# Two passes instead of three in the output and down projection: the operand's high and low part side by side in one matmul of 512 columns

## The chip, the cores and the metric

The kernel runs on one core of a Trainium2 chip. The metric is the device time of one execution in microseconds (us). The engines are named as in the profile: PE (TensorE, the matmuls), PEld (its weight loads), DVE (VectorE), ACT (ScalarE), POOL (GpSimd) and SP (which issues the DMAs).

## What is computed

One layer of a decoder trunk, for 256 tokens of 2048 features, in float32:

```
h   = rms_norm(x) * gain + shift                 # gain, shift, g1, g2: c (1 x 2048) through w_ada
p   = h @ w_in                                   # 52 tiles of 128 columns
mix = [retention(p) | rwkv7(p) | moba(p)]        # 4 + 4 + 8 tiles of 128 features
x1  = x + g1 * (mix @ w_out)
h2  = rms_norm(x1) * gain + shift
u,v = conv3(h2 @ w_up)                           # 2 x 44 tiles of 128 columns
x2  = x1 + g2 * ((silu(u) * v) @ w_down)
out = rms_norm(x2)
```

## The kernel before

Features lie on the partitions and the 256 tokens along the free axis. All four products run tile by tile: a weight tile of 128 x 128 is the stationary operand, a feature tile of 128 x 256 (all tokens) the moving one, and the sum over feature tiles is kept in a PSUM bank. To keep float32 accuracy with the faster matmul type (float32r), weights and operands are both split into a high and a low part, and each weight tile takes three matmuls of 256 columns: high weight by high operand (line 1182), high weight by low operand (L1183), low weight by high operand (L1184). The product of both low parts is left out. A bank holds 512 float32 values on each partition; these products use its first half.

The weights come as a stream in the order of use, cut into chunks of 8 tiles (24 matmuls). For each chunk ACT writes the high part (`hi`, L454) and DVE the rest (`lo`, L455); `convert_until` does this two chunks ahead, into three buffers of each. There are 400 chunks: 104 for the input product, 32 for the output product (256 tiles), 176 for the up and 88 for the down product (704 tiles). Between the weights the stream also brings the 96 blocks of `w_ada`, which `ada_block` multiplies by the condition and sums on DVE (L408, 128 x 2048 elements each): the scales and shifts that the next norms need.

The operand of the output product comes from the three mixers. Retention and MoBA are done early; RWKV's steps alternate with chunks of the output product, and the hook at the 21st chunk waits until RWKV is finished. `split` writes the two parts of the result (`mxhi` with ACT, `mxlo` with DVE, L423 and L424). A column tile of the output product is summed in two parts, so there are 32 evacuations (`evac_out`, L1028, DVE: x = mm * g1 + x). The second of each is followed by the sum of squares for the next norm (`norm_acc`: ACT squares, POOL adds, and DVE does the last addition, L1042).

At the end of the output product the order is this. The first 64 tiles of the up product (8 chunks) work with x * gain before the norm is known (`xghi`, `xglo`, 258 columns). Meanwhile DVE finishes the sum of squares (`acc`), PE takes the mean (`nps`), DVE works out 1/sqrt in twelve small steps (`rsqrt`, L231 to L236), PE and ACT spread the result (`rs`), and DVE and ACT make the operand of the rest of the up product (`xn` and `hlo`, L434 and L436) and scale the early tiles (L1076). Then come the up product's other chunks with `hhi` and `hlo`.

The operand of the down product is `ghi` and `glo`, its 16 column tiles are summed over 44 feature tiles each without a break, and `evac_down` (L1123) ends each one.

The program is written as one loop over the chunks (L1156 on). A scheduler then puts each engine's instructions in a fixed order, by its own estimate of when each could run; each engine executes its own list in that order. So the order of `lo`, `ada` blocks, evacuations and norm steps on DVE is not written by hand, and it changes when the program changes.

Of the kernel before, what the change touches and what calls it, by code (L numbers as in the profile page):

```python
# [8 lines left out]
F32 = mybir.dt.float32  # L9
# [14 lines left out]
# input projection tiles, 128 columns each: 0-15 RWKV (r, k, v, [wd, wa, wg, wg]),  # L24
# 16-27 retention (q, k, v, g), 28-51 MoBA (q, k, v of a head side by side)
# [33 lines left out]
    # input projection: S tiles stay open over all k, a k tile at a time; others are visited for some k tiles  # L59
# [29 lines left out]
    # output projection: retention and half of MoBA, then the other half of MoBA, and RWKV  # L89
# [68 lines left out]
# parts of w_ada, blocks of 128 channels  # L158
ADA = {"mix_shift": 0, "mix_gain": 16, "g1": 32, "ffn_shift": 48, "ffn_gain": 64, "g2": 80}
RAWB, EXTRA, CONVB, AHEAD = 3, 2, 3, 2  # L160
# blocks of the modulation in the last part of the input projection, four of the output and three of the up projection
LATE_ADA = (18, 3, 3, 2, 0, 7, 7, 8)
# column pairs of the up projection that begin with x * gain, before the norm of x is known
EARLY = 8
# chunks of the output projection that wait for MoBA, for RWKV, and that begin the FFN; steps of the mixers per chunk
WAITS = (7, 20, 28)
TASKS = 5
# blocks of weights that may wait in the arena, up to a chunk
# [3 lines left out]
def trunk(tc, A):  # L172
# [12 lines left out]
    # one piece of memory in turn for more blocks of weights, the mixers, and the up projection  # L185
# [16 lines left out]
    def s4(name, dt=F32):  # L202
        return arena.tile([128, 4, T], dt, tag="s4", name=nm(name))

# [21 lines left out]
    def rsqrt(x, w):  # L226
        """x ** -0.5 on [128, w], three Newton steps from an integer estimate."""
# [11 lines left out]
    # ---- constants and vectors  # L239
# [16 lines left out]
    # ---- x, its mean square, and x / rms  # L256
# [4 lines left out]
    # ---- the stream of weights  # L261
# [17 lines left out]
    def begun(m, f):  # L279
        """blocks of a product before the first tile of k tile f or later"""  # L280
# [29 lines left out]
    def lead():  # L310
        """blocks of weights that may wait in the arena"""
# [3 lines left out]
    def place(it):  # L315
        """memory for the next block, in one piece or two; None while it is all in use"""
# [29 lines left out]
    # silu(c) along the free axis of all partitions  # L346
# [24 lines left out]
    def norm_bcast(ms, name):  # L371
        """rms of the tokens (mean squares in ms[:, 0:2]) -> 1/rms on all partitions, [128, 256] in PSUM"""
# [26 lines left out]
    # ---- modulation: w_ada has its output channels on the partitions  # L399
# [870 lines left out]
```

## Time and profile before

| | |
|---|---|
| runs (device time of one execution) | 1331.02, 1331.79, 1333.01 us; median 1331.79 |
| the profiled execution, first to last instruction (span) | 1329.3 us |
| PE busy | 1290.8 us, 97% |
| DVE busy | 1034.6 us, 78% |
| ACT busy | 648.6 us, 49% |
| output product, first to last matmul | 397.9 to 552.4 us |
| early tiles of the up product (258 columns), up to | 577.8 us |
| other tiles of the up product, up to | 1061 us |
| down product, up to | 1314 us |
| last norm and store | 1314 to 1329.3 us |

The profile gives the profiled execution's span alone. The median of the timed runs is 2.5 us above it, so a change of the span by d puts the median at about 1331.8 + d. Times within the span are us from its first instruction. A matmul's recorded duration (0.28 us) is longer than the distance to the next one, since consecutive matmuls overlap; the distance between two starts is what a matmul costs in a row of them.

### The profile page before, as it was taken

To read this page: it belongs to the slowest core of one execution; us is meant where nothing else is said; L and a number is where in the kernel's file an instruction comes from. 1 tells how busy PE (TensorE), PEld (TensorE's weight loads), DVE (VectorE), ACT (ScalarE), POOL (GpSimd) and SP (SyncE) were. 2 spreads that over 40 slices of the span, in tenths; PEclk is the share of its full clock that TensorE was granted. 3 is DMA by queue.
4 is the path that set the end of the run, shared out by engine and by line. 5 is a ranking of instruction groups with operands and counts; after the bars stand their busy time and mean duration, and the time that the engine had idled before them with its cause. 6 is when DMAs were issued, how large, how long until landed. Compare 5 with 4: busy or idle time off the path is not lost.

```text
span 1329.3 us, 25320 instructions
## 1 busy us (share of the span) xinstructions
PE 1290.8 (97%) x10524; PEld 1272.4 (96%) x10524; DVE 1034.6 (78%) x1606; ACT 648.6 (49%) x1043; POOL 40.2 (3%) x41
## 2 busy tenths in 40 slices
PE   5899999999999999999999999999999999999996
PEld 5899999999999999999999999999999999999995
DVE  7888989999897579999777898888866666566444
ACT  3454435566346324565445655656554544434341
POOL 0000000000000001400000000000000000000000
PEclk8999999999999899999999999999999999999998
DMA  9998887775537279677775565565655577767551
GB/s 386 365 349 317 314 316 286 285 271 194 217 128 253 96 251 402 210 281 297 270 285 188 173 210 191 190 210 175 219 190 183 206 247 270 267 241 271 187 191 64
DMA packets 49939, 320.56 MB, mean 241 GB/s; under 512 B 5536, under 2 KB 6048, under 8 KB 15776
## 3 DMA queue, kind: packets, MB, share of 16 engines
q1 hardware_dynamic: 48528, 315.10, 66.2%
q0 software_dynamic: 1008, 3.67, 0.7%
q8 instruction: 82, 1.34, 0.4%
q14 instruction: 33, 0.27, 0.1%
q10 hardware_dynamic: 288, 0.17, 0.0%
HBM read 316.83 MB, written 2.10 MB: 240 GB/s over the span
## 4 chain that ended last, share of the span: by engine, by line
PE 90%; DVE 7%; issue 2%; ACT 1%; DMA 0%; POOL 0%; DVEq 0%; ACTq 0%; POOLq 0%
PE mm L1182 26%; PE mm L1184 26%; PE mm L1183 26%; DVE raw L408 2%; DVE lo L455 1%; PE pair L1182 1%; PE pair L1184 1%; PE pair L1183 1%; PE xx L774 1%; PE sp L919 1%; PE sp L933 1%; PE u L911 1%; PE akv L784 0%; PE yps L913 0%; PE xx L775 0%
## 5 line engine op out<-in xcount | busy, mean ns | idle before, releaser
L455 DVE TENSOR_TENSOR lo<-raw,hi 128x1024 fp32r<-128x1024 f32 x400 | 488.7, 1224 | 201.9 <-ACT hi L454 200.8
L454 ACT CAST hi<-raw 128x1024 fp32r<-128x1024 f32 x400 | 418.3, 1047 | 449.5 <-PE mm L1183 373.3
L1182 PE MATMUL mm<-hhi,hi 128*128 128x256 f32 x2016 | 571.7, 284 | 0.0
L1184 PE MATMUL mm<-hhi,lo 128*128 128x256 f32 x2016 | 571.1, 283 | 0.5 <-DVE lo L455 0.5
L1183 PE MATMUL mm<-hlo,hi 128*128 128x256 f32 x2016 | 571.3, 283 | 0.0
L1184 PEld LDWEIGHTS mm<-hhi,lo 128*128 128x128 f32 x2016 | 386.6, 192 | 1.3 <-DVE lo L455 0.9
L1182 PEld LDWEIGHTS mm<-hhi,hi 128*128 128x128 f32 x2016 | 386.8, 192 | 0.6 <-issue 0.3
L1183 PEld LDWEIGHTS mm<-hlo,hi 128*128 128x128 f32 x2016 | 386.8, 192 | 0.3
L408 DVE SCALAR_TENSOR_TENSOR raw<-raw,cb 128x2048 f32<-128x2048 f32 x96 | 221.7, 2310 | 5.2 <-DMA raw<-w_ada 5.2
L1184 PE MATMUL mm<-ghi,lo 128*128 128x256 f32 x704 | 199.1, 283 | 0.0
L1182 PE MATMUL mm<-ghi,hi 128*128 128x256 f32 x704 | 198.8, 282 | 0.0
L1183 PE MATMUL mm<-glo,hi 128*128 128x256 f32 x704 | 198.5, 282 | 0.0
L1183 PEld LDWEIGHTS mm<-glo,hi 128*128 128x128 f32 x704 | 134.6, 191 | 0.0
L1182 PEld LDWEIGHTS mm<-ghi,hi 128*128 128x128 f32 x704 | 134.5, 191 | 0.0
L1184 PEld LDWEIGHTS mm<-ghi,lo 128*128 128x128 f32 x704 | 134.4, 191 | 0.0
L1182 PE MATMUL mm<-mxhi,hi 128*128 128x256 f32 x256 | 75.1, 293 | 1.0 <-DVE x L1028 0.9
L1184 PE MATMUL mm<-mxhi,lo 128*128 128x256 f32 x256 | 73.2, 286 | 0.4 <-DVE lo L455 0.4
L1183 PE MATMUL mm<-mxlo,hi 128*128 128x256 f32 x256 | 73.5, 287 | 0.0
L1042 POOL TENSOR_TENSOR acc<-acc,nsq 128x256 f32<-128x256 f32 x28 | 34.2, 1221 | 848.8 <-ACT nsq L1041 848.6
L1182 PE MATMUL pair<-hhi,hi 128*128 128x256 f32 x160 | 45.7, 298 | 7.1 <-ACT hi L454 5.2
L1182 PEld LDWEIGHTS mm<-mxhi,hi 128*128 128x128 f32 x256 | 49.7, 194 | 2.8 <-DVE x L1028 1.1
L1184 PEld LDWEIGHTS mm<-mxhi,lo 128*128 128x128 f32 x256 | 49.7, 194 | 0.5 <-DVE lo L455 0.5
(292 smaller groups left out, 1304.8 us busy)
## 6 DMA issues: line engine op xcount, KB each, us to landing
raw<-w_ada SPq DMA_DIRECT2D x96, 1024.0 KB, 5.1
raw<-w_up SPq DMA_DIRECT2D x67, 1024.0 KB, 4.9
raw<-w_in SPq DMA_DIRECT2D x52, 1024.0 KB, 5.8
raw<-w_down SPq DMA_DIRECT2D x44, 1024.0 KB, 5.0
raw<-w_up SPq DMA_DIRECT2D x42, 512.0 KB, 8.3
raw<-w_out SPq DMA_DIRECT2D x18, 512.0 KB, 8.8
raw<-w_out SPq DMA_DIRECT2D x7, 1024.0 KB, 4.9
x<-xT SPq DMA_DIRECT2D x4, 512.0 KB, 5.5
```

The costliest lines, as they stand in the source:

```text
L408: V.scalar_tensor_tensor(raw, raw, 1.0, cb, op0=OP.mult, op1=OP.mult, accum_out=m)
L454: S.copy(flat(hi), src)
L455: V.tensor_tensor(flat(lo), src, flat(hi).bitcast(F32), op=OP.subtract)
L774: PE.matmul(ps[:, T * i:T * i + 128], L[pb, f, sl], At[pb, f, sl], start=True, stop=True)
L911: PE.matmul(ups[pb, 128 * f:128 * f + 128], M1[:, f, ts], sb[:, f], start=True, stop=True)
L919: PE.matmul(sp[:, fs], kT[pb, h, fs], vT[pb, h, fs], start=(f == 0), stop=False, skip_group_check=True)
L933: PE.matmul(sp[:, fs], bT[pb, h, fs], U[pb, h, fs], start=False, stop=True, skip_group_check=True)
L1042: (V if t == NF - 1 else G).tensor_tensor(norm["acc"], norm["acc"], sq, op=OP.add)
L1182: PE.matmul(ps, whi[:, j], hi, start=first and not (two and t % 2), stop=False, skip_group_check=two)
L1183: PE.matmul(ps, whi[:, j], lo, start=False, stop=False, skip_group_check=two)
L1184: PE.matmul(ps, wlo[:, j], hi, start=False, stop=last, skip_group_check=two)
```

## The change

`pairs` lays the high and the low part of a feature tile next to each other, so that both are one run of 512 columns. In the output and down products (`WIDE`) the high weight tile is then loaded once and multiplied by all 512 columns, into a whole bank; the low weight tile still takes the 256 columns of the high part, into the bank's first half. Two matmuls and two weight loads stand where three and three stood, with as many columns in all. The evacuation adds the two halves of the bank to x one after the other, so it takes two DVE instructions instead of one. `split` writes RWKV's share in two pieces instead of one, since a pair of feature tiles is now one buffer. Input and up product only address their operand differently.

```diff
+WIDE = ("out", "down")
...
+    def pairs(name, tile_of=None):
+
+        shape = lambda x: x.rearrange("p (f h) t -> p f h t", h=2)
+        return [shape((tile_of or s4)(name, F32R)) for _ in range(2)]
...
     def split(g, sl, src):
...
         if g not in MX:
-            MX[g] = s4("mxhi", F32R), s4("mxlo", F32R)
-        hi, lo = (flat(x)[:, sl] if isinstance(sl, slice) else x[:, :, sl[0]] for x in MX[g])
-        S.copy(hi, src)
-        V.tensor_tensor(lo, src, hi.bitcast(F32), op=OP.subtract)
+            MX[g] = pairs("mx")
+        f, n, ts = sl
+        while n:
+            w = min(n, 2 - f % 2)
+            x = MX[g][f // 2][:, f % 2:f % 2 + w]
+            hi, lo = x[:, :, 0, ts], x[:, :, 1, ts]
+            S.copy(hi, src[:, 0:w])
+            V.tensor_tensor(lo, src[:, 0:w], hi.bitcast(F32), op=OP.subtract)
+            src = src[:, w:]
+            f, n = f + w, n - w
...
     def evac_out(t, part, ps):
         dst = x1[t // 4][:, t % 4]
-        V.scalar_tensor_tensor(dst, ps, mod["g1"][:, t:t + 1], dst, op0=OP.mult, op1=OP.add)
+        for h in range(2):
+            V.scalar_tensor_tensor(dst, ps[:, T * h:T * h + T], mod["g1"][:, t:t + 1], dst, op0=OP.mult, op1=OP.add)
...
     def evac_down(t, part, ps):
         dst = x1[t // 4][:, t % 4]
-        V.scalar_tensor_tensor(dst, ps, mod["g2"][:, t:t + 1], dst, op0=OP.mult, op1=OP.add)
+        for h in range(2):
+            V.scalar_tensor_tensor(dst, ps[:, T * h:T * h + T], mod["g2"][:, t:t + 1], dst, op0=OP.mult, op1=OP.add)
...
-            PE.matmul(ps, whi[:, j], hi, start=first and not (two and t % 2), stop=False, skip_group_check=two)
-            PE.matmul(ps, whi[:, j], lo, start=False, stop=False, skip_group_check=two)
-            PE.matmul(ps, wlo[:, j], hi, start=False, stop=last, skip_group_check=two)
+            if m in WIDE:
+
+                x = operands(m, k)
+                PE.matmul(ps.rearrange("p (h t) -> p h t", h=2), whi[:, j], x, start=first, stop=False,
+                          skip_group_check=True)
+                PE.matmul(ps[:, 0:T], wlo[:, j], x[:, 0], start=False, stop=last, skip_group_check=True)
+            else:
...
```

The scheduler's order changes with it, at three places. In the rows below `mm` is a bank of a product, `mx`, `xg` and `h` its operands (of the output product, of the up product's first and of its other tiles), `hi` and `lo` the weights, `raw` a block as loaded, and numbers tell buffers apart.

PE, at the end of the output product, where the up product's first tiles follow; before:

```order
L1182 MATMUL mm_6203<-mxhi_5208,hi_6110 128x256
L1183 MATMUL mm_6203<-mxlo_5209,hi_6110 128x256
L1184 MATMUL mm_6203<-mxhi_5208,lo_6111 128x256
L1182 MATMUL mm_6251<-xghi,hi_6148 128x258
L1183 MATMUL mm_6251<-xglo,hi_6148 128x258
```

and now:

```order
L1199 MATMUL mm_5985<-mx_5153,hi_5908 128x512
L1201 MATMUL mm_5985<-mx_5153,lo_5909 128x256
L1204 MATMUL mm_6031<-xghi,hi_5940 128x258
L1205 MATMUL mm_6031<-xglo,hi_5940 128x258
L1206 MATMUL mm_6031<-xghi,lo_5941 128x258
```

A tile of the output product has two matmuls instead of three; the up product keeps three. Over the program PE has 960 matmuls and as many weight loads fewer, one for each of the 256 + 704 tiles. Also, 141 of the 256 tiles stood ahead of RWKV's last transposes (`yt`) on PE before, and 170 do now.

DVE, at the last evacuations of the output product; before:

```order
L1028 SCALAR_TENSOR_TENSOR x_4723<-mm_6165,mod_g_160,x_4723 128x256
L455 TENSOR_TENSOR lo_6187<-raw_5641,hi_6186 128x1024
L1028 SCALAR_TENSOR_TENSOR x_4723<-mm_6190,mod_g_160,x_4723 128x256
L1028 SCALAR_TENSOR_TENSOR x_4723<-mm_6203,mod_g_160,x_4723 128x256
L416 TENSOR_TENSOR mod_ffn_shift<-mod_ffn_shift,vec 128x1
L455 TENSOR_TENSOR lo_6225<-raw_5677,hi_6224 128x1024
L1042 TENSOR_TENSOR acc_5803<-acc_5803,nsq_6221 128x256
```

and now:

```order
L468 TENSOR_TENSOR lo_5973<-raw_5530,hi_5972 128x1024
L1042 SCALAR_TENSOR_TENSOR x_4723<-mm_5976,mod_g_160,x_4723 128x256
L1042 SCALAR_TENSOR_TENSOR x_4723<-mm_5985,mod_g_160,x_4723 128x256
L1042 SCALAR_TENSOR_TENSOR x_4723<-mm_5976,mod_g_160,x_4723 128x256
L1042 SCALAR_TENSOR_TENSOR x_4723<-mm_5985,mod_g_160,x_4723 128x256
L468 TENSOR_TENSOR lo_6005<-raw_5559,hi_6004 128x1024
L1056 TENSOR_TENSOR acc_5656<-acc_5656,nsq_6001 128x256
```

Each tile is evacuated twice. From RWKV's last split up to the last evacuation DVE's list had 18 evacuations, 5 `ada` blocks, 13 `lo` of weights, 5 `xglo` and 4 small instructions; it now has 32, 1, 11, 5 and none.

DVE, within the norm's twelve small steps, which follow; before:

```order
L235 TENSOR_TENSOR rsa_6234<-rsa_6234,m_6231 128x2
L408 SCALAR_TENSOR_TENSOR raw_6318,mod_ffn_gain<-raw_6318,cb 128x2048
L236 SCALAR_TENSOR_TENSOR rsy_6233<-rsa_6234,rsy_6233 128x2
L455 TENSOR_TENSOR lo_6283<-raw_5678,hi_6282 128x1024
L234 SCALAR_TENSOR_TENSOR rsa_6234<-rsy_6233 128x2
L455 TENSOR_TENSOR lo_6325<-raw_5744,hi_6324 128x1024
L235 TENSOR_TENSOR rsa_6234<-rsa_6234,m_6231 128x2
L410 SCALAR_TENSOR_TENSOR mod_ffn_gain<-mod_ffn_gain,bias_164,vec 128x1
L236 SCALAR_TENSOR_TENSOR rsy_6233<-rsa_6234,rsy_6233 128x2
```

and now:

```order
L415 SCALAR_TENSOR_TENSOR raw_6098,mod_ffn_gain<-raw_6098,cb 128x2048
L241 SCALAR_TENSOR_TENSOR rsa_6014<-rsy_6013 128x2
L468 TENSOR_TENSOR lo_6206<-raw_5740,hi_6205 128x1024
L242 TENSOR_TENSOR rsa_6014<-rsa_6014,m_6011 128x2
L468 TENSOR_TENSOR lo_6245<-raw_5741,hi_6244 128x1024
L243 SCALAR_TENSOR_TENSOR rsy_6013<-rsa_6014,rsy_6013 128x2
L417 SCALAR_TENSOR_TENSOR mod_ffn_gain<-mod_ffn_gain,bias_164,vec 128x1
L241 SCALAR_TENSOR_TENSOR rsa_6014<-rsy_6013 128x2
L415 SCALAR_TENSOR_TENSOR raw_6199,mod_ffn_shift<-raw_6199,cb 128x2048
L242 TENSOR_TENSOR rsa_6014<-rsa_6014,m_6011 128x2
L415 SCALAR_TENSOR_TENSOR raw_6280,mod_ffn_gain<-raw_6280,cb 128x2048
L243 SCALAR_TENSOR_TENSOR rsy_6013<-rsa_6014,rsy_6013 128x2
```

`ada` blocks have moved from ahead of the last evacuation to behind it. From the last evacuation up to the `lo` of the third chunk that needs `hhi`, DVE's list had 2 `ada` blocks, 9 `lo`, 13 `xn` and `hlo`, 4 scalings of early tiles, `acc` and 14 small instructions; it now has 7, 9, 14, 4, one and 19. The step `rs` on PE, which waits for the last of the twelve, has moved: 75 of the 258-column matmuls stood between the last matmul of the output product and it, now 129 do.

## Rows read from the trace of the kernel before

**Rows 1.** The page, busy time of the engines, share of the span, instructions.

```profile
PE 1290.8 (97%) x10524; PEld 1272.4 (96%) x10524; DVE 1034.6 (78%) x1606; ACT 648.6 (49%) x1043; POOL 40.2 (3%) x41
```

**Rows 2.** The page, shares of the chain that ended last, by engine.

```profile
PE 90%; DVE 7%; issue 2%; ACT 1%; DMA 0%; POOL 0%; DVEq 0%; ACTq 0%; POOLq 0%
```

**Rows 3.** Stretches: length, busy us of PE, PEld, DVE, ACT, POOL; clock, DMA share.

```profile
513.60:553.30 39.70, 38.75 (x321) 38.36 (x320) 39.01 (x52) 21.10 (x32) 16.75 (x13) 1.00 0.87 331
600.00:700.00 100.00, 100.00 (x836) 100.00 (x835) 79.41 (x93) 50.89 (x80) 0.00 (x0) 1.00 0.77 279
1200.00:1300.00 100.00, 100.00 (x838) 100.00 (x837) 50.97 (x48) 40.88 (x48) 6.42 (x6) 1.00 0.59 200
```

**Rows 4.** The chain by line, window 531 to 553 us.

```profile
by line: DVE lo L455 34.6%; issue 24.4%; DVE x L1028 19.7%; DVE raw L408 16.5%; ACT hi L454 4.8%; DVE mod_ffn_gain L410 1.4%; DVE mod_ffn_shift L416 1.0%
```

**Rows 5.** The chain by line, window 1061 to 1314 us (down projection).

```profile
by line: PE mm L1184 33.5%; PE mm L1182 33.3%; PE mm L1183 33.3%
```

**Rows 6.** Timeline, down projection, PE and PEld: start, us, what.

```profile
1150.02 0.28 PE L1183 MATMUL mm<-glo,hi 128*128 128x256 f32 x1
1150.02 0.19 PEld L1184 LDWEIGHTS mm<-ghi,lo 128*128 128x128 f32 x1
1150.14 0.28 PE L1184 MATMUL mm<-ghi,lo 128*128 128x256 f32 x1
1150.14 0.19 PEld L1182 LDWEIGHTS mm<-ghi,hi 128*128 128x128 f32 x1
```

**Rows 7.** Timeline, PE, plain float32 matmuls.

```profile
415.21 1.06 PE L858 MATMUL y<-R,bd 128*128 128x128 f32 x8
416.10 0.60 PE L603 MATMUL mo_o<-mo_ptb,mo_vs 128*128 128x256 f32 x2
```

**Rows 8.** DVE groups by form, window 513.6 to 553.3 us: busy, mean ns.

```profile
L455 DVE TENSOR_TENSOR lo<-raw,hi 128x1024 fp32r<-128x1024 f32 x13 | 16.3, 1255 | 0.3 <-ACT hi L454 0.3
L408 DVE SCALAR_TENSOR_TENSOR raw<-raw,cb 128x2048 f32<-128x2048 f32 x5 | 12.8, 2570 | 0.0
L1028 DVE SCALAR_TENSOR_TENSOR x<-mm,mod_g,x 128x256 f32<-128x256 f32 x18 | 8.3, 472 | 0.4 <-PE mm L1184 0.4
```

**Rows 9.** Timeline, PE, end of the output and start of the up projection.

```profile
552.39 0.28 PE L1184 MATMUL mm<-mxhi,lo 128*128 128x256 f32 x1
...
577.78 0.28 PE L1182 MATMUL mm<-hhi,hi 128*128 128x256 f32 x1
...
583.54 0.28 PE L1182 MATMUL mm<-hhi,hi 128*128 128x256 f32 x1
```

**Rows 10.** Timeline, DVE, from the last evacuation of the output projection on.

```profile
552.76 0.47 DVE L1028 SCALAR_TENSOR_TENSOR x<-mm,mod_g,x 128x256 f32<-128x256 f32 x1
...
555.64 0.43 DVE L1042 TENSOR_TENSOR acc<-acc,nsq 128x256 f32<-128x256 f32 x1 [0.62 <-POOL acc L1042]
556.82 0.16 DVE L374 TENSOR_SCALAR m<-nps 128x2 f32<-128x2 f32 x1 [0.76 <-PE nps L1046]
557.02 0.17 DVE L231 TENSOR_SCALAR rsy<-m 128x2 int32<-128x2 int32 x1
557.22 0.17 DVE L232 TENSOR_SCALAR rsy<-rsy 128x2 int32<-128x2 int32 x1
...
557.70 2.28 DVE L408 SCALAR_TENSOR_TENSOR raw<-raw,cb 128x2048 f32<-128x2048 f32 x1
...
564.80 0.88 DVE L434 SCALAR_TENSOR_TENSOR xn<-x,mod_ffn_gain,rs_ffn 128x256 f32<-128x256 f32 x2
565.59 1.22 DVE L1076 TENSOR_TENSOR up<-up,rs_ffn 128x1024 f32<-128x1024 f32 x1
...
573.20 1.22 DVE L455 TENSOR_TENSOR lo<-raw,hi 128x1024 fp32r<-128x1024 f32 x1 [0.17 <-ACT hi L454]
...
581.50 2.35 DVE L455 TENSOR_TENSOR lo<-raw,hi 128x1024 fp32r<-128x1024 f32 x2
```

**Rows 11.** Timeline, DVE, the last evacuation of the down projection.

```profile
1314.51 0.48 DVE L1123 SCALAR_TENSOR_TENSOR x<-mm,mod_g,x 128x256 f32<-128x256 f32 x1 [6.45 <-PE mm L1184]
```

More of the change, by code (lines that the diff above doesn't have):

```diff
@@ L429, in h_tile @@
         if g not in H:
-            H[g] = s4("hhi", F32R), s4("hlo", F32R)
-        hi, lo = H[g]
+            H[g] = pairs("h")
+        hi, lo = (H[g][j // 2][:, j % 2, i] for i in range(2))
         gain, shift = (mod[kind + n][:, f:f + 1] for n in ("_gain", "_shift"))
@@ L434, in h_tile @@
         V.scalar_tensor_tensor(xn, XN[kind][g][:, j], gain, RS[kind], op0=OP.mult, op1=OP.mult)
-        S.activation(hi[:, j], xn, AF.Identity, bias=shift)
-        V.scalar_tensor_tensor(lo[:, j], xn, shift, hi[:, j].bitcast(F32), op0=OP.add, op1=OP.subtract)
+        S.activation(hi, xn, AF.Identity, bias=shift)
+        V.scalar_tensor_tensor(lo, xn, shift, hi.bitcast(F32), op0=OP.add, op1=OP.subtract)
     hooks = {}
@@ L556, in retention @@
             done()
-            split(0, slice(512 * hh, 512 * hh + 512), flat(mixed[:, 2 * hh:2 * hh + 2]))
+            split(0, (2 * hh, 2, slice(0, T)), mixed[:, 2 * hh:2 * hh + 2])
             yield 1 - hh
@@ L605, in moba @@
         yield
-        split(g, slice(T * (h % 4), T * (h % 4) + T), o[:, 0:256])
+        split(g, (h % 4, 1, slice(0, T)), o[:, None, 0:256])
         done()
@@ L976, in rwkv @@
             done()
-            split(1, (sl,), mixed[:, :, sl])
+            split(1, (0, 4, sl), mixed[:, :, sl])
             yield
@@ L1114, in evac_up @@
         if g not in GT:
-            first = lambda n: tail[0].tile([128, 4, T], F32R, tag="gt", name=nm(n))
-            GT[g] = (first("ghi"), first("glo")) if g < 2 else (s4("ghi", F32R), s4("glo", F32R))
-        hi, lo = GT[g]
-        S.copy(hi[:, j], v)
-        V.tensor_tensor(lo[:, j], v, hi[:, j].bitcast(F32), op=OP.subtract)
+            first = lambda n, dt: tail[0].tile([128, 4, T], dt, tag="gt", name=nm(n))
+            GT[g] = pairs("g", first if g < 2 else s4)
+        hi, lo = (GT[g][j // 2][:, j % 2, i] for i in range(2))
+        S.copy(hi, v)
+        V.tensor_tensor(lo, v, hi.bitcast(F32), op=OP.subtract)
     def evac_down(t, part, ps):
         dst = x1[t // 4][:, t % 4]
-        V.scalar_tensor_tensor(dst, ps, mod["g2"][:, t:t + 1], dst, op0=OP.mult, op1=OP.add)
+        for h in range(2):
+            V.scalar_tensor_tensor(dst, ps[:, T * h:T * h + T], mod["g2"][:, t:t + 1], dst, op0=OP.mult, op1=OP.add)
         norm_acc(t, dst)
@@ L1138, in operands @@
             k = RANK[k]
-        hi, lo = src[k // 4]
-        return hi[:, k % 4], lo[:, k % 4]
+        return src[k // 4][k % 4 // 2][:, k % 2]
     evac = {"in": evac_in, "out": evac_out, "up": evac_up, "down": evac_down}
@@ L1178, in trunk @@
             early = m == "up" and t % NP < EARLY and k < 4
-            ps = opened[t][:, 0:T + 2] if early else opened[t][:, 0:T]
-            hi, lo = (x[:, k] for x in XG) if early else operands(m, k)
+            ps = opened[t] if m in WIDE else opened[t][:, 0:T + 2] if early else opened[t][:, 0:T]
             two = t in both
-            PE.matmul(ps, whi[:, j], hi, start=first and not (two and t % 2), stop=False, skip_group_check=two)
-            PE.matmul(ps, whi[:, j], lo, start=False, stop=False, skip_group_check=two)
-            PE.matmul(ps, wlo[:, j], hi, start=False, stop=last, skip_group_check=two)
+            opens = first and not (two and t % 2)
+            if m in WIDE:
[4 more added lines that the diff above has]
+            else:
+                hi, lo = (x[:, k] for x in XG) if early else (operands(m, k)[:, i] for i in range(2))
+                PE.matmul(ps, whi[:, j], hi, start=opens, stop=False, skip_group_check=two)
+                PE.matmul(ps, whi[:, j], lo, start=False, stop=False, skip_group_check=two)
+                PE.matmul(ps, wlo[:, j], hi, start=False, stop=last, skip_group_check=two)
             if last:
```

## The prediction, made before the changed kernel ran

> **What bounds the kernel now.** First the page: PE is busy 97% of the span [rows 1] and holds 90% of the chain that ended last, DVE 7% [rows 2]. An average hides the stages, so next the stretches: from 600 us on PE is busy 100% and DVE has slack, while between RWKV's last split (513.6) and the last evacuation of the output product (553.3) DVE is busy 39.0 of 39.7 us [rows 3]. There the chain's largest shares are DVE's: the weights' `lo`, the evacuations, the `ada` blocks [rows 4]. In the down product the chain is PE's three matmul lines, a third each, and nothing else [rows 5]. So two stages are to be judged: down, where a nanosecond per tile on PE is a nanosecond of the end, times 704; and the passage from output to up product, where DVE's list decides. In these stretches the granted clock is 1.00 [rows 3], the 2.4 GHz level, at which 256 columns at one per cycle would take 106.7 ns.
>
> **The down product.** Matmuls start 0.12 us apart, and the next weights' load starts together with each matmul [rows 6]; the stretch of 100 us with 838 recorded matmuls [rows 3] gives 119.3 ns, a few missing records aside, so I use 120. A tile is 3 x 120 = 360 ns now. Afterwards it is one pass of 512 columns plus one of 256, the latter 120 as now. No float32r pass of 512 columns stands in the trace, so I bound it. Above: twice a pass, 240, if the 13.3 ns over 106.7 go with the columns. Below: the nearest row with as many cycles is plain float32 with 256 columns, which streams at half the rate: two of them last 0.60 us, one record of such is 0.38, so 0.22 lies between them, while eight with 128 columns last 1.06 us, (1.06 - 0.28) / 7 = 0.11 apiece [rows 7]. From 0.11 to 0.22 the stream doubles, and what lies over 106.7 and 213.3 is 3 to 7 ns in both: there the excess belongs to the instruction, not to the columns. So I take a fixed excess: 213.3 + 13.3 = 227 ns, a tile of 347, 13.3 ns saved, 704 x 13.3 = **-9.4 us**. The ends are a tile of 216 + 120 = 336 (24 ns, -16.9 us), with the float32 row's excess alone, and 360 (0).
>
> The Trainium skill ("TensorE: Matmul & The Clock Gate", section "Back-to-back issue gap") gives N/2.4 + 2.5 ns for the gap at full clock, 216 ns for 512 columns. It also gives 109 for 256, where the rows above show 120, so applied to both passes it would leave only 2.5 ns per tile, 1.8 us in the stage, to be saved.
>
> Evacuations in down go from 16 to 32. DVE is half idle there [rows 3], so all but the last are hidden; the cover would be gone only if DVE filled. The last tile's second instruction lies on the path to the final norm: one costs 0.47 to 0.48 us [rows 10, 11], **+0.4** for a second behind it.
>
> **The output product and its passage to the up product.** PE alone would save 256 x 13.3 = 3.4 us here. But the end of this stage is set by DVE, whose list is the same set of work in another order. I go through it in two pieces.
>
> *RWKV's split to the last evacuation.* On PE 170 tiles instead of 141 now stand ahead of RWKV's last transposes. The extra 29 cost 29 x 0.347 = 10.1 us, the other 141 save 141 x 0.0133 = 1.9, so RWKV's split comes 8.2 later, near 521.8. After it, DVE's list loses 4 `ada` blocks of 2.57 us, 2 `lo` of 1.26 and four small instructions, and gains 14 evacuations of 0.47 [rows 8]: 39.0 - 10.3 - 2.5 - 0.8 + 6.6 = 32.0. The last evacuation ends near 521.8 + 32.0 = 553.8 instead of 553.2 [rows 10]: **+0.6**. PE's own work would let it end 3.4 earlier, which bounds this term below; the pieces of RWKV's split and waits put its upper end at about +3.
>
> *The last evacuation to the third chunk that needs the normed operand.* Before, DVE ended the last evacuation at 553.2 and the third chunk's `lo` (the first of the pair that starts at 581.50) at 582.7, 29.5 us later [rows 10]. PE came to that chunk at 583.54 and to its third matmul, the first that reads `lo`, 0.24 later [rows 9]: a reserve of 1.1 us, no more. The list now holds 5 more `ada` blocks in this piece. One takes 2.2 us of the queue (2.28 recorded, less its overlap with the next) [rows 10]. With one more `xn` (0.88 for two, so 0.4) and five small steps (0.2 between starts) [rows 10] that is 11.0 + 0.4 + 1.0 = 12.4 us, while what PE does meanwhile is the same 190 early matmuls and two chunks. Each `ada` block stands between dependent steps of 1/sqrt, so it delays `rs`, then the operand, then the `lo` behind them; the waits for POOL and PE of 0.62 and 0.76 us [rows 10] come ahead of most of them and hide one block at best in part. What is late next is PE: it should stand first at `rs`, then at the first chunks of `hhi`. Shift: 12.4 - 1.1 = **+11.3**. After that the up product is PE alone at 100% [rows 3] with its three passes unchanged, and never gets this back. The blocks that were taken forward are missing later, where DVE had slack: nothing gained. The extra 32 evacuations and the two pieces of the split are counted in the lists above; DMAs are the same in number.
>
> **Sum.** -9.4 + 0.4 + 0.6 + 11.3 = +2.9 us on the profiled execution's span of 1329.3, 1332.2. The runs' median, 1331.8, lies 2.5 above the span; with the same difference **1334.7 us**. A measurement of this kernel can tell about 0.2%, 2.7 us, from no change: 1329.1 to 1334.5 counts as the same, so this sits on the edge of it.
>
> **Rivals.**
> 1. *The excess goes with the columns* (0 to 4 ns saved per tile). For it: 256-column passes show 13 ns over the stream where float32 shows 3 to 7, and what differs is the rate at which the operand is read. Against: the float32 rows' fixed excess. Then down gives 0 to -2.8, RWKV's split comes about 10 later, the last evacuation +2, and the passage still +11.3: 1331.8 - 1.4 + 0.4 + 2 + 11.3 = 1344.
> 2. *The excess is that of the load beside the stream and vanishes behind a long pass* (336 ns a tile): the kernel is faster. The place is down: 704 x 24 = -16.9. The split comes 29 x 0.336 - 141 x 0.024 = 6.4 later, the last evacuation at 552.0, -1.2; passage +11.3, tail +0.4: 1331.8 - 6.4 = 1325.4. It decides from 17 ns per tile on, where the saving in down passes the delay. For it: the load starts with the matmul and is recorded for 0.19 us, longer than the 0.12 between them [rows 6]. Against: it would have to be the load alone, while plain float32 with the same loads runs at 0.11.
> 3. *The DVE delay is absorbed*: the added blocks run in gaps that the list doesn't show, and PE never stands. Then -3.4 - 9.4 + 0.4: 1319.4. Against it: DVE is nearly full just before [rows 3], the list is executed in order, and the reserve is 1.1 us.
> 4. *The change doesn't do what it says*: excluded, since the instruction lists hold 960 matmuls fewer.
>
> The formula of the Trainium skill quoted above, taken for the pass of 512 columns alone beside the measured 120, gives rival 2's time, 1325; since it misses the measured 256-column gap by 11 ns, I give that case no more for it.
>
> **Chances.** Forecast 0.43 (1331 to 1339 by the bounds of the evacuation term and of the waits), rival 1 0.27, rival 2 0.23, rival 3 0.05, and 0.02 for none of these. Of the forecast's share 0.24 lies above 1334.5, 0.17 in the band and 0.02 below it. Slower: 0.24 + 0.27 + 0.01 = 0.52. Same: 0.17 + 0.02 of rival 2 = 0.19. Faster: 0.02 + 0.21 + 0.05 + 0.01 = 0.29. Range: from the lower half of rival 2 to rival 1's upper bound, 1323 to 1346; rival 3 and the fringes stay outside.
>
> **What would show it.** In the profile after: the distance between a 512-column start and the next in down (227 here; 236 to 240 by rival 1, 216 by rival 2), and 347 ns per tile, so a stage of 704 x 0.347 = 244 us. PE idle near 565 to 600 us, first before `rs` (waiting for DVE's `rsy`), then before `hhi` chunks (waiting for ACT's and DVE's `hi`, `lo` and operand), some 11 to 14 us in all, with 6 `ada` blocks on DVE just ahead; by rival 3 none. The last evacuation of output within 3 us of 553. The forecast is wrong if PE runs through that stretch, or if a tile of down takes under 340 or over 353 ns.

## The result and the profile after

The changed kernel took **1343.0 us** (median of 4 runs, 1341.4 to 1343.5), the kernel before 1331.7 beside it: ratio 1.0084, 95% interval 1.0069 to 1.0098. It is slower, beyond the 0.2% that can be told. The profiled execution has a span of 1341.6 us, 12.3 more than before, with 960 matmuls fewer (the medians lie 11.3 apart: the profile before is of the quickest of its runs, this one of the slowest of its four):

```profile
PE 1288.8 (96%) x9564; PEld 1224.5 (91%) x9564; DVE 1050.8 (78%) x1656; ACT 649.9 (48%) x1045; POOL 40.1 (3%) x41
```

PE is busy 2.0 us less than before [rows 1] and idle 14.3 us more, so the added time is waiting. To find the place I put the two timelines side by side by stages. All numbers are us from the span's start, read from first and last starts:

| | before | after | difference |
|---|---|---|---|
| first matmul of the output product | 397.9 | 400.6 | +2.7 |
| RWKV's last transposes on PE | 509.2 | 519.5 | +10.3 |
| last evacuation of the output product ends | 553.2 | 558.3 | +5.1 |
| first `hhi` tile of the up product | 577.8 | 593.9 | +16.1 |
| first matmul of the down product | 1061.6 | 1077.8 | +16.2 |
| last matmul of the down product | 1314.2 | 1326.0 | +11.8 |
| end | 1329.3 | 1341.6 | +12.3 |

The down product got 4.4 us shorter, the rest of the way lost 16. In five stretches of the passage (length, busy us of PE, PEld, DVE, ACT, POOL; granted clock, DMA share) DVE is busy nearly all the time from 565 to 585 us while PE stands, and the granted clock falls to 0.51 after PE has been idle:

```profile
505.00:520.00 15.00, 15.00 (x89) 13.02 (x88) 13.84 (x29) 5.32 (x7) 0.00 (x0) 1.00 1.02 413
520.00:530.00 10.00, 6.74 (x31) 5.56 (x30) 7.33 (x18) 3.93 (x7) 0.00 (x0) 0.83 1.02 417
565.00:575.00 10.00, 8.28 (x69) 8.07 (x67) 9.87 (x20) 3.17 (x3) 0.00 (x0) 1.00 0.72 268
575.00:585.00 10.00, 3.21 (x13) 2.92 (x14) 10.00 (x18) 2.60 (x11) 0.00 (x0) 0.51 0.77 301
585.00:595.00 10.00, 9.26 (x63) 9.05 (x63) 7.53 (x12) 6.00 (x16) 0.00 (x0) 0.81 1.02 387
```

Before the change PE was idle for about 1 us in the same place, all of it ahead of 565 us, and the granted clock stayed at 1.00:

```profile
555.00:575.00 20.00, 18.96 (x156) 18.60 (x155) 17.81 (x37) 12.96 (x35) 0.60 (x1) 1.00 0.71 261
575.00:585.00 10.00, 10.00 (x86) 10.00 (x85) 10.00 (x12) 7.12 (x17) 0.00 (x0) 1.00 0.63 229
```

The waits of PE in the changed kernel, from its timeline (the last bracket names how long PE was idle and whom it waited for):

```profile
523.77 0.59 PE L1199 MATMUL mm<-mx,hi 128*128 128x512 f32 x1 [3.26 <-DVE mx L435]
...
578.95 1.23 PE L385 MATMUL rs<-cst,rsy 128*128 128x128 f32 x4 [5.67 <-DVE rsy L243]
583.02 0.58 PE L1204 MATMUL mm<-xghi,hi 128*128 128x258 f32 x1 [2.84 <-ACT c L1105]
```

The second row is the wait that the prediction named: PE stands 5.67 us before `rs`, for the last step of 1/sqrt. DVE's timeline shows what filled its queue:

```profile
556.39 1.89 DVE L1042 SCALAR_TENSOR_TENSOR x<-mm,mod_g,x 128x256 f32<-128x256 f32 x4
...
560.47 2.28 DVE L415 SCALAR_TENSOR_TENSOR raw<-raw,cb 128x2048 f32<-128x2048 f32 x1
...
565.57 2.28 DVE L415 SCALAR_TENSOR_TENSOR raw<-raw,cb 128x2048 f32<-128x2048 f32 x1
...
569.13 2.29 DVE L415 SCALAR_TENSOR_TENSOR raw<-raw,cb 128x2048 f32<-128x2048 f32 x1
...
574.25 2.29 DVE L415 SCALAR_TENSOR_TENSOR raw<-raw,cb 128x2048 f32<-128x2048 f32 x1
...
576.53 2.29 DVE L415 SCALAR_TENSOR_TENSOR raw<-raw,cb 128x2048 f32<-128x2048 f32 x1
...
578.74 0.15 DVE L243 SCALAR_TENSOR_TENSOR rsy<-rsa,rsy 128x2 f32<-128x2 f32 x1
...
579.01 2.29 DVE L415 SCALAR_TENSOR_TENSOR raw<-raw,cb 128x2048 f32<-128x2048 f32 x1
...
598.51 2.35 DVE L468 TENSOR_TENSOR lo<-raw,hi 128x1024 fp32r<-128x1024 f32 x2
```

From the last evacuation's end (558.3) to the `lo` of the third `hhi` chunk (598.51 + 1.2 = 599.7) DVE needs 41.4 us, where it had needed 29.5 [rows 10]. Six `ada` blocks (L415) lie before 582 us, and the last step of 1/sqrt is over at 578.9, 20.6 us after the evacuation; before, it was over at 563.3, 10 us after.

PE's third wait was not in the prediction. ACT too runs its list in order; it reached the copy of `rs` early and stood there 7.41 us, and the copies that empty the banks of the early tiles (L1103, L1105) were behind it:

```profile
580.21 0.37 ACT L395 COPY rs_ffn<-rs 128x256 f32<-128x256 f32 x1 [7.41 <-PE rs L385]
...
582.55 0.35 ACT L1103 COPY up<-mm 128x256 f32<-128x256 f32 x1
```

So PE, after `rs`, had no free bank and waited another 2.84 us, and then worked at the low clock (0.51 on average from 575 to 585 us). It came to the third `hhi` chunk at 593.9 + 48 x 0.12 = 599.7, when that chunk's `lo` was ready: two chains that end at the same time.

For the down product, one row of each kernel gives 704 tiles, with the first and last start of the high-weight pass. Before:

```profile
L1182 PE MATMUL mm<-ghi,hi x704: 278/283/286, 1061.6 to 1314.0; 128*128 128x256 f32 x176
```

After:

```profile
L1199 PE MATMUL mm<-g,hi x704: 388/398/403, 1077.8 to 1325.7; 128*128 128x512 f32 x176
```

(1314.0 - 1061.6) / 703 = 359.0 ns a tile before, (1325.7 - 1077.8) / 703 = 352.6 after: 6.4 saved. In the timeline the 512-column pass takes 0.24 and the 256-column pass 0.12 here:

```profile
1150.06 0.40 PE L1199 MATMUL mm<-g,hi 128*128 128x512 f32 x1
1150.30 0.28 PE L1201 MATMUL mm<-g,lo 128*128 128x256 f32 x1
1150.42 0.40 PE L1199 MATMUL mm<-g,hi 128*128 128x512 f32 x1
```

### The profile page after: what moved, and what is told of

It is laid out like the page before. It is cut to its first block, busy times and chain, and to the rows that moved or that the text cites. A ratio compares the mean times of both kernels' runs of the same rounds, so it can differ in the third digit from the quotient of the medians.

```text
span 1341.6 us, 23430 instructions
## 1 busy us (share of the span) xinstructions
PE 1288.8 (96%) x9564; PEld 1224.5 (91%) x9564; DVE 1050.8 (78%) x1656; ACT 649.9 (48%) x1045; POOL 40.1 (3%) x41
## 4 chain that ended last, share of the span: by engine, by line
PE 55%; DVE 1%; ACT 0%; DVEq 0%; issue 0%; ACTq 0%
PE mm L1199 12%; PE mm L1204 12%; PE mm L1205 12%; PE mm L1206 12%; PE mm L1201 6%; DVE x L1146 0%; PE rs L385 0%; DVE x L1138 0%; DVEq L1287 0%; PE ms L1060 0%; DVE rsa L242 0%; DVE rsy L243 0%; DVE rsa L241 0%; DVE acc L1056 0%; ACT nsq L1055 0%
## 5 line engine op out<-in xcount | busy, mean ns | idle before, releaser
L1204 PE MATMUL mm<-h,hi 128*128 128x256 f32 x2016 | 571.9, 284 | 0.5 <-ACT hi L467 0.5
L1206 PE MATMUL mm<-h,lo 128*128 128x256 f32 x2016 | 571.1, 283 | 1.0 <-DVE lo L468 1.0
L1205 PE MATMUL mm<-h,hi 128*128 128x256 f32 x2016 | 571.3, 283 | 0.0
L1206 PEld LDWEIGHTS mm<-h,lo 128*128 128x128 f32 x2016 | 386.7, 192 | 1.7 <-DVE lo L468 1.4
L1204 PEld LDWEIGHTS mm<-h,hi 128*128 128x128 f32 x2016 | 386.8, 192 | 1.3 <-ACT hi L467 0.7
L1205 PEld LDWEIGHTS mm<-h,hi 128*128 128x128 f32 x2016 | 386.8, 192 | 0.3
L1199 PE MATMUL mm<-g,hi 128*128 128x512 f32 x704 | 248.4, 398 | 0.0
L415 DVE SCALAR_TENSOR_TENSOR raw<-raw,cb 128x2048 f32<-128x2048 f32 x96 | 220.1, 2293 | 4.9 <-DMA raw<-w_ada 3.7
L1201 PE MATMUL mm<-g,lo 128*128 128x256 f32 x704 | 197.8, 281 | 0.0
L1199 PEld LDWEIGHTS mm<-g,hi 128*128 128x128 f32 x704 | 132.3, 188 | 32.5
L1201 PEld LDWEIGHTS mm<-g,lo 128*128 128x128 f32 x704 | 133.0, 189 | 0.0
L1199 PE MATMUL mm<-mx,hi 128*128 128x512 f32 x256 | 95.4, 410 | 4.8 <-DVE mx L435 3.3
L1204 PE MATMUL pair<-h,hi 128*128 128x256 f32 x160 | 45.6, 297 | 6.7 <-ACT hi L467 4.8
L1205 PE MATMUL pair<-h,hi 128*128 128x256 f32 x160 | 46.2, 292 | 0.0
```

The lines of the kernel that those rows point to most:

```text
L415: V.scalar_tensor_tensor(raw, raw, 1.0, cb, op0=OP.mult, op1=OP.mult, accum_out=m)
L1199: PE.matmul(ps.rearrange("p (h t) -> p h t", h=2), whi[:, j], x, start=first, stop=False, skip_group_check=True)
L1201: PE.matmul(ps[:, 0:T], wlo[:, j], x[:, 0], start=False, stop=last, skip_group_check=True)
L1204: PE.matmul(ps, whi[:, j], hi, start=opens, stop=False, skip_group_check=two)
L1205: PE.matmul(ps, whi[:, j], lo, start=False, stop=False, skip_group_check=two)
L1206: PE.matmul(ps, wlo[:, j], hi, start=False, stop=last, skip_group_check=two)
```

## The experiments

Two things were to be explained: where the 16 us come from, and why a tile saved half of what was forecast. **Theory A**: the scheduler's order of DVE's list, `ada` blocks behind the last evacuation, causes the passage's delay. The rivals B to E put it on the change's own work: the wide passes, the second evacuations, DVE's total. Each ratio is to the kernel before, timed on the same chip.

### 1. The layout alone

```diff
-WIDE = ("out", "down")
+WIDE = ()
...
-        for h in range(2):
+        for h in range(2 if "out" in WIDE else 1):
...
-        for h in range(2):
+        for h in range(2 if "down" in WIDE else 1):
```

> The new operand layout and RWKV's split in two pieces, but three passes of 256 columns and one evacuation per tile everywhere, as before. Its list on DVE has five ada blocks between the last evacuation of the output product and the end of 1/sqrt, as the changed kernel has, and one was there before. Theory A (the delay comes from the order of DVE's list behind the last evacuation): the passage costs 11 to 12 us more than before, nothing is saved in down: 1343 us (1341 to 1346), PE idle at rs. Theory B (the delay comes from the wide passes or the second evacuations of the output product): the time of before, 1331.7.

Measured: 1340.0 us, ratio 1.0069 (1.0052 to 1.0086). No wide pass and no second evacuation is in it, and yet it is 8.8 us slower than the kernel before. PE's waits in its passage are the changed kernel's, a little shorter:

```profile
572.62 1.22 PE L385 MATMUL rs<-cst,rsy 128*128 128x128 f32 x4 [4.70 <-DVE rsy L243]
576.48 0.58 PE L1204 MATMUL mm<-xghi,hi 128*128 128x258 f32 x1 [2.65 <-ACT c L1105]
```

The first `hhi` tile starts at 586.6, 8.8 us later than before; from the last matmul of the output product (550.5) to it are 36.1 us, 25.4 before. The median is 1 us below the range that was expected. Theory A stands, B falls: another operand layout and a split in two pieces, with every pass and evacuation as before, were enough for the scheduler to choose another list.

### 2. The down product alone, with the old split

```diff
-WIDE = ("out", "down")
+WIDE = ("down",)
...
-            MX[g] = pairs("mx")
...
+            MX[g] = s4("mxhi", F32R), s4("mxlo", F32R)
+        f, n, ts = sl
+        hi, lo = (x[:, f:f + n, ts] for x in MX[g])
+        S.copy(hi, src)
+        V.tensor_tensor(lo, src, hi.bitcast(F32), op=OP.subtract)
```

> Only the down product is wide; the output product's operand, split and evacuation are as before, and DVE's list up to the down product has the same counts as before. Theory A, with the 6.7 ns per tile that the changed kernel's trace shows: down 704 x 6.7 = 4.7 us shorter, 0.4 to 0.5 for the second evacuation of the last tile: 1331.7 - 4.2 = 1327.5 us, faster (1326.5 to 1328.5). By the fixed excess of the prediction, 13.3 ns: 1322.8. Theory B': the wide passes delay something else in down: 1331.7 or more.

Measured: 1327.1 us, ratio 0.9976 (0.9964 to 0.9988), as theory A has it. The row of the high-weight pass gives (1307.6 - 1059.6) / 703 = 352.8 ns a tile, the changed kernel's price:

```profile
L1196 PE MATMUL mm<-g,hi x704: 388/398/403, 1059.6 to 1307.6; 128*128 128x512 f32 x176
```

The wide passes are a small gain where the list in front of them stays as it was.

### 3. The blocks held behind the norm

```diff
-        V.scalar_tensor_tensor(raw, raw, 1.0, cb, op0=OP.mult, op1=OP.mult, accum_out=m)
+        s = PINNED[0][:, 0:1] if PINNED else 1.0
+        V.scalar_tensor_tensor(raw, raw, s, cb, op0=OP.mult, op1=OP.mult, accum_out=m)
...
         XN["ffn"] = x1
+        one = tiny("one", 1)
+        V.tensor_scalar(one, RS["ffn"][:, 0:1], 0.0, 1.0, op0=OP.mult, op1=OP.add)
+        PINNED.append(one)
```

> The changed kernel, but each ada block issued after the norm takes its factor 1.0 from a value computed from the norm's result, so that it can't be put ahead of it: DVE's list then has no ada block between the last evacuation and the end of 1/sqrt, and three up to the third chunk of the up product, instead of five and two. Theory A: 4 fewer blocks of 2.2 us and the earlier rs give 9 to 12 us back, and PE no longer falls to the lower clock: 1331 to 1335 us. Theory B: no change from the changed kernel, 1343.

Measured: 1338.8 us, ratio 1.0047 (1.0031 to 1.0063): 4 us back, not 9 to 12. The passage itself did what theory A says. PE's wait for `rs` fell from 5.67 us to 0.17:

```profile
565.38 0.68 PE L385 MATMUL rs<-cst,rsy 128*128 128x128 f32 x4 [0.17 <-DVE rsy L243]
```

From the last matmul of the output product to the first `hhi` tile it took 25.1 us (557.4 to 582.5), before the change 25.4. But the gain was partly paid back. Two stretches, with the columns as above, show how:

```profile
555.00:575.00 20.00, 19.75 (x156) 19.04 (x156) 18.09 (x38) 13.62 (x32) 3.64 (x4) 1.00 0.15 54
600.00:610.00 10.00, 5.74 (x46) 5.53 (x45) 7.97 (x10) 3.70 (x9) 0.00 (x0) 0.97 1.02 415
```

From 555 to 575 us the DMAs are busy 15% (71% before the change). The blocks that wait occupy the buffers, so little is loaded; the longest wait of the DMA queue for a block to be worked off (the last number; 9.4 us before the change) was 36.0 us in the window from 540 to 615 us:

```profile
SPq L345 <- DVE raw L417: 66.1, 7, 36.0
```

At 600 us PE is idle 4.3 us of ten, while ACT stands 6.67 us for an operand that is behind those blocks on DVE:

```profile
606.30 0.51 ACT L450 ACTIVATE h<-xn,mod_ffn_shift 128x256 fp32r<-128x256 f32 x1 [6.67 <-DVE xn L449]
```

From the first `hhi` tile to the first matmul of the down product it took 490.5 us (582.5 to 1073.0), in the changed kernel 483.9: 6.6 of the 11.4 us that the passage had won were lost again. So the expectation was wrong in taking the waiting blocks to be free.

### 4. One evacuation in the output product

```diff
     def evac_out(t, part, ps):
...
-        for h in range(2):
+        for h in range(1):
```

> The changed kernel with one evacuation per tile in the output product: the second half of its banks (the product of high weights and low operand) is left out of the result. Both products run wide on PE. DVE's list behind the last evacuation then has one and one ada blocks, as before. Theory A: no passage delay; out saves 256 x 6.7 = 1.7, down 4.7 less 0.4: 1331.7 - 6.0 = 1325.7 (1324 to 1329). Theory C (PE's wide passes in the output product cause the delay through RWKV, not the list): about 1340.

Measured: 1325.3 us, ratio 0.9957 (0.9942 to 0.9972). With one block each in the two pieces of the list, as before, the delay in the passage is gone (last matmul of the output product 549.8, first `hhi` tile 574.7: 24.9 us), with all wide passes in place. Theory C falls.

### 5. The output product alone

```diff
-WIDE = ("out", "down")
+WIDE = ("out",)
...
-        for h in range(2):
+        for h in range(2 if "down" in WIDE else 1):
```

> Only the output product is wide (with its two evacuations); the down product has three passes and one evacuation as before. DVE's list up to the down product has the same counts as the changed kernel's. Theory A with additive parts: the changed kernel's 1343.0 plus the 4.7 that its down product saved, less 0.5 for the last second evacuation: 1347.2 us (1345.5 to 1349). Theory D (the delay needs both parts): under 1342.

Measured: 1348.4 us, ratio 1.0132 (1.0117 to 1.0147), within the range of theory A. The parts add up: the wide output product with its list costs 17.6 us, the wide down product gives 5.4 of them back.

### 6 and 7. The blocks moved ahead, into the input product

```diff
-LATE_ADA = (18, 3, 3, 2, 0, 7, 7, 8)
+LATE_ADA = (24, 4, 4, 0, 0, 1, 7, 8)
```

and, in the second kernel, `(26, 3, 3, 0, 0, 1, 7, 8)`.

> The changed kernel with other numbers of ada blocks in the stream: 24, 4, 4, 0, 0, 1, 7, 8 instead of 18, 3, 3, 2, 0, 7, 7, 8, so that six more come with the last part of the input product and six fewer with the first part of the up product. DVE's list: one block behind the last evacuation up to the third chunk of the up product, where the changed kernel has seven; PE's order around RWKV's last transposes as in the changed kernel (339 and 340 matmuls of the output product ahead of them). Theory A: the passage is as before the change, 11 to 12 us back: 1331 to 1332.5 us, with what is left of the delay in front of RWKV's last split. Theory E (the second evacuations fill DVE, wherever the blocks stand): 1341 to 1343, since DVE does as much in all.

> As the run beside it, with 26, 3, 3, 0, 0, 1, 7, 8: one block behind the last evacuation, and the scheduler puts 311 instead of 340 of the output product's matmuls ahead of RWKV's last transposes. Theory A: the passage's 11 to 12 us come back, and of the 4 us in front of RWKV's last split some 3 as well: 1326 to 1330 us. By theory E 1341 to 1343.

Measured: 1347.4 us, ratio 1.0119 (1.0093 to 1.0145), and 1355.5, ratio 1.0194 (1.0146 to 1.0242). Both expectations of the total were wrong, that of the passage was right: from the last matmul of the output product to the first `hhi` tile it took 24.6 us (574.7 to 599.3) and 24.8 (578.0 to 602.8), over 12 less than in the changed kernel. But the output product began at 424.1 and 439.3 instead of 400.6. In the first of the two, PE's low-weight passes of the input product waited 5.7 us for `lo`, 0.5 in the changed kernel:

```profile
L1206 PE MATMUL mm<-h,lo 128*128 128x256 f32 x466 | 133.9, 288 | 5.7 <-DVE lo L468 5.7
```

The mixers' steps also went further ahead of the output product there, which then took 151 and 139 us instead of 156. Part of the delay is the clock: between 240 us and the start of the output product the granted clock was 0.83, 0.91 and 0.91 in three stretches of 20 us of the first (from 240, 320 and 400 us), and 0.74, 0.91, 0.57 and 0.91 in four of the second (from 240, 320, 360 and 420), where the changed kernel shows 1.00 in all. By these numbers that is about 7 and 17 us, an estimate; PE was also idle 8 and 11 us more than in the changed kernel between 60 and 440 us. So the two totals don't give the price of the blocks' place alone. Theory E is half right: the blocks have to run somewhere on DVE. In the kernel before five ran between RWKV's last split and the last evacuation, beside half as many evacuations, and 17 behind the passage, from 583 to 700 us, where PE didn't wait. That the five would cost nothing there too is not shown by any run.

### 8. Two passes of 512 columns

```diff
+                if m == "down":
+                    PE.matmul(ps.rearrange("p (h t) -> p h t", h=2), wlo[:, j], x, start=False, stop=last,
+                              skip_group_check=True)
+                else:
+                    PE.matmul(ps[:, 0:T], wlo[:, j], x[:, 0], start=False, stop=last, skip_group_check=True)
```

> The changed kernel, but in the down product the low weights too are multiplied by all 512 columns (the product of both low parts, which is left out otherwise, is added). Two passes of 512 columns per tile tell the price of such a pass: by a fixed excess of 13.3 ns 227 each and 453 a tile, a stage of 319 us; by an excess that goes with the columns 240 and 480, 338 us; by the split that the changed kernel's trace suggests (235.4 for 512 columns, 117.3 for 256: about half fixed and half by columns, 6.7 ns each per 256) 233 and 467, 329 us. The run's time: 1343 plus the stage's growth over 248 us.

Measured: 1413.5 us (one run). The row gives (1395.8 - 1075.4) / 703 = 455.8 ns a tile, 228 a pass, and the timeline starts 0.22 to 0.23 apart:

```profile
L1199 PE MATMUL mm<-g,hi x704: 387/389/400, 1075.4 to 1395.8; 128*128 128x512 f32 x176
```

```profile
1150.13 0.39 PE L1199 MATMUL mm<-g,hi 128*128 128x512 f32 x1
1150.36 0.39 PE L1202 MATMUL mm<-g,lo 128*128 128x512 f32 x1
1150.58 0.39 PE L1199 MATMUL mm<-g,hi 128*128 128x512 f32 x1
```

That is the 227 of the prediction, the fixed excess of 13.3 ns, and neither of the others. So the price was right for a 512-column pass that follows another, and wrong for one between 256-column passes.

### 9 and 10. Grouped passes, and the other half of the bank

Both start from the kernel of experiment 2. In the first:

```diff
-                PE.matmul(ps[:, 0:T], wlo[:, j], x[:, 0], start=False, stop=last, skip_group_check=True)
+                low.append((ps[:, 0:T], wlo[:, j], x[:, 0], last))
...
+        for ps, w, x, last in low:
+            PE.matmul(ps, w, x, start=False, stop=last, skip_group_check=True)
         for t, part, ps in ready:
```

In the second the low-weight pass writes `ps[:, T:2 * T]`.

> The kernel with only the down product wide and the old split, but in down the eight high-weight passes of a chunk (512 columns each) come first and its eight low-weight passes (256 columns) after them, so that passes of one length follow each other. If a 512-column pass costs more beside a 256-column one (235 where they alternate, 227 to 228 where 512 follows 512), a tile falls from 352.7 ns to 228 + 120 = 348: the stage to about 245 us, 3.5 us less than ungrouped: 1323.5 us. If each length has its price wherever it stands (235.4 and 117.3), as ungrouped: 1327.1.

> The kernel with only the down product wide and the old split, but the low-weight pass adds into the bank's second half instead of the first; the sum of both halves is the same. If the 512-column pass is slowed because the pass before it wrote the half that it begins with, a tile falls from 352.7 ns towards 347 and the run to 1323.5 us; if the place in the bank doesn't matter, 352.7 ns and 1327.1.

Measured: grouped 1323.9 us, ratio 0.9951 (0.9938 to 0.9964); with the other half 1329.8, ratio 0.9978 (0.9968 to 0.9989). Grouping helps: the stage's first to last start is 246.0 us (1059.6 to 1305.6) against 248.2 in experiment 2 (1059.6 to 1307.8), 3 ns a tile of the 4.7 expected, and it is the fastest of the complete kernels tried. In its timeline (a row of n passes lasts n - 1 distances and one duration)

```profile
1149.83 1.31 PE L1196 MATMUL mm<-g,hi 128*128 128x512 f32 x5
1150.98 1.11 PE L1212 MATMUL mm<-g,lo 128*128 128x256 f32 x8
1151.93 0.86 PE L1196 MATMUL mm<-g,hi 128*128 128x512 f32 x3
```

five 512-column passes lie (1.31 - 0.40) / 4 = 0.228 us apart, three others (0.86 - 0.40) / 2 = 0.23, and eight of 256 columns (1.11 - 0.28) / 7 = 0.119. Over the whole stage a tile takes (246.0 + 0.12) / 704 = 349.6 ns, which less 119 leaves 231 for a 512-column pass, so that even in a group it doesn't come to 228 throughout. The half of the bank makes no difference: 1064.1 to 1312.3, 248.2 us again. Its median is no reading of the place in the bank either: its program is the same as experiment 2's up to the down product, and its ratio to before is the same within the interval.

## Why the prediction was right or wrong

The side (slower), the mechanism and the place were forecast, and 1343.0 lies in the range; but the size, +2.9 us, was a quarter of what came, +12.3 on the span. The forecast's own bounds, 1331 to 1339, don't hold 1343.0; it lies in the range because rival 1's bound, 1346, was taken in, and that the range held is luck as far as the forecast goes. By its steps:

- **The last evacuation to the third `hhi` chunk: +11.3.** Right. DVE took 41.4 us where 29.5 + 12.4 = 41.9 were forecast, and the first `hhi` tile comes 35.6 us after the last evacuation instead of 24.6: +11.0. Experiments 1, 3 and 4 show that the `ada` blocks in the list are the cause: from the output product's last matmul to the first `hhi` tile it took 36.0 to 37.2 us in every kernel with five blocks between the last evacuation and the end of 1/sqrt (the changed one, experiments 1, 5 and 8), and 24.6 to 25.4 in every one with at most one there (before, 2, 3, 4, 6, 7, 9, 10), whichever passes were wide. Only the second half of PE's waiting had another form: it waited for banks behind ACT's wait for `rs` and ran at the low clock, not for `lo`. From 565 to 595 us its idle time is 9.3 us, where 11 to 14 were named.
- **The down product: -9.4.** The step that failed is the price of a 512-column pass. 227 ns holds where passes of 512 follow each other (228, experiment 8). Between passes of 256 columns it takes about 352.6 - 119 = 234, if a 256-column pass takes 119 as in experiment 9 (the starts of the changed kernel's trace are 235.4 and 117.3 ns apart on average). The saving is 6.4 ns a tile and 4.4 us, between the forecast's case and rival 1 (0 to 4 ns). I priced each pass by itself and added; the experiments show that the price depends on the neighbours. Why is not settled: the place in the bank is excluded by experiment 10, and grouping recovers 3 of the 6 ns. The tile of 352.6 ns lies just inside the prediction's own sign of being wrong, 353.
- **RWKV's split to the last evacuation: +0.6.** The other step that failed: it came +5.1. I counted 29 tiles moved ahead of RWKV's last transposes (+8.2) and no wait. Measured at the transposes: +10.3, of which 2.7 was there when the output product began. 1.0 of these was there at the very first matmul of the input product (23.7 instead of 22.7 us), which the change doesn't touch, and experiments 2 and 10, with one program up to the down product, began the output product 1.5 us apart (398.9 and 400.4). The other 7.6 are the moved tiles and the clock. At the measured prices the tiles come to 170 x 0.3526 - 141 x 0.359 = 9.3 us. The granted clock was below 1.00 in both profiles, first before, then after:

```profile
440.00:480.00 40.00, 40.00 (x293) 37.27 (x292) 24.71 (x51) 11.43 (x23) 0.00 (x0) 0.91 0.42 156
```

```profile
480.00:500.00 20.00, 20.00 (x124) 16.73 (x124) 12.08 (x19) 5.73 (x12) 0.00 (x0) 0.91 0.70 238
```

  That is an estimated 0.09 x 40 = 3.6 us lost before and 1.8 after, and 7.6 + 3.6 - 1.8 = 9.4. So the cost of the moved tiles was right but for the price of a pass; what was wrong was the wait put at nothing. Behind the transposes PE had two tiles left (from 519.56 to 520.5 us) and then waited 3.26 us for the split (its row stands above, at 523.77), with the granted clock at 0.83 in that stretch. Before, it went on without a wait. DVE's last steps of RWKV took hardly longer than before, 5.9 us from the start of `yc` to the end of the split instead of 5.7. Before:

```profile
507.98 0.69 DVE L964 TENSOR_TENSOR yc<-yc,rsy 128x512 f32<-128x512 f32 x1
...
512.95 0.68 DVE L424 TENSOR_TENSOR mxlo<-mix_rwkv,mxhi 128x512 fp32r<-128x512 f32 x1
```

  After:

```profile
518.39 0.69 DVE L977 TENSOR_TENSOR yc<-yc,rsy 128x512 f32<-128x512 f32 x1
519.00 2.29 DVE L415 SCALAR_TENSOR_TENSOR raw<-raw,cb 128x2048 f32<-128x2048 f32 x1
...
521.21 0.60 DVE L986 SCALAR_TENSOR_TENSOR mix_rwkv<-yt,vec,rwm 128x128 f32<-128x128 f32 x2
...
523.85 0.43 DVE L435 TENSOR_TENSOR mx<-mix_rwkv,mx 128x256 fp32r<-128x256 f32 x1
```

  An `ada` block stands there now, but in the place of two `lo` of 1.2 us. So the wait comes from the 29 tiles: moved ahead of the transposes, they were missing as work for PE during these steps. Experiment 6 agrees: with 339 matmuls ahead of the transposes and no `ada` block in these steps PE waited too, 1.78 us, and in experiment 7, with 311, it didn't. The 1.5 us between the two waits may be the block's.

```profile
543.25 0.50 PE L1199 MATMUL mm<-mx,hi 128*128 128x512 f32 x1 [1.78 <-DVE mx L435]
```

  From the split's end (524.3) to the last evacuation DVE took 34.0 us, 32.0 forecast. It was busy for 30.5 of them; the rest is waiting, the longest, 2.26 us, for PE's first tiles behind the split. The forecast also set 39.0 us, DVE's busy time, for a stretch that had lasted 39.6; with 39.6 the step would have been +1.2.
- **The tail: +0.4.** Right: +0.5 (12.3 at the end, 11.8 at the last matmul).
- **Rivals.** Rival 2 (336 ns) is excluded by every run with a wide down product (349.6 is the least, in experiment 9); rival 3 (the delay absorbed) by PE's 5.67 us before `rs`. Rival 1 hit the time, 1344, with half of its reason: the tile saved more than its 0 to 4 ns, and the evacuation came later than its +2.
- **The formula of the Trainium skill** ("TensorE: Matmul & The Clock Gate", section "Back-to-back issue gap"), which the page gives for the gap of an isolated matmul, 216 ns for 512 columns, doesn't hold for these float32r passes: the lowest mean of a stage is 228, in experiment 8.

Sum of the corrections: the down product 5.0 and the last evacuation 4.5, together 9.5, which is the 9.4 between +2.9 and +12.3.

## What to carry to other kernels

Where a scheduler orders an engine's list, compare the whole lists at every stage border before costing an edit: here a new operand layout with a split in two pieces, even without any change on PE, let the scheduler put five blocks of 2.2 us among dependent steps, which cost more than the edit could save. Add up what stands between the last producer and the next consumer on that engine, and look at the steps ahead of it too: work that is moved ahead of a dependent step no longer covers that step. The edit itself pays where it leaves the lists alone: the down product alone, with the passes of a chunk grouped by length, gives 0.5%.

## What the runs showed of the hardware that was not expected

- A float32r pass of 512 columns takes 228 ns after another of 512, and 234 to 235 between passes of 256, by the same reckoning as above.
- Nearly all of what a tile takes beyond one column per cycle is gone at the lower clock (1.2 GHz, granted clock 0.50). There one tile of 512 + 256 columns took 0.65 us in the changed kernel, where 768 columns at 1.2 GHz come to 0.640; at 2.4 GHz they come to 320 ns, and the tile took 352.6.

```profile
524.10:527.40 3.30, 3.30 (x12) 2.76 (x11) 1.01 (x3) 1.04 (x1) 0.00 (x0) 0.50 1.01 415
```

```profile
524.36 0.63 PE L1199 MATMUL mm<-mx,hi 128*128 128x512 f32 x1
...
525.01 0.63 PE L1199 MATMUL mm<-mx,hi 128*128 128x512 f32 x1
```

- PE's granted clock falls in some executions of the same program in RWKV's steps, between 440 and 480 us, while PE is recorded as busy all the time. Experiments 2 and 10 have the same program there. Experiment 2:

```profile
440.00:460.00 20.00, 20.00 (x160) 18.27 (x159) 9.46 (x16) 6.80 (x16) 0.00 (x0) 1.00 0.26 88
460.00:480.00 20.00, 20.00 (x161) 18.47 (x160) 16.80 (x39) 6.64 (x10) 0.00 (x0) 1.00 0.74 283
```

  and experiment 10 (clock 0.92 and 0.91, and fewer matmuls done in as many us):

```profile
440.00:460.00 20.00, 20.00 (x146) 18.14 (x145) 8.72 (x14) 5.92 (x14) 0.00 (x0) 0.92 0.19 66
460.00:480.00 20.00, 20.00 (x149) 18.80 (x148) 15.54 (x36) 5.44 (x6) 0.00 (x0) 0.91 0.57 211
```

  At RWKV's last transposes they are 4.4 us apart (507.2 and 511.6), 1.5 of them since the start of the output product, and that is the size of the spread within the runs of one kernel (1325.6 to 1330.5 in experiment 2, 1328.9 to 1333.7 of the kernel before). A difference of 0.3% between two single profiles of this kernel therefore says nothing; stages must be compared within a profile, and medians over several runs.
